# Three edits to one kernel: two stores moved behind loads on one DMA queue, and one product moved to another PSUM tile

## The chip, the cores and the metric

The kernel runs on one core of a Trainium2 chip. A core has a matrix engine (TensorE, PE in the profile), a vector engine (VectorE, DVE), a scalar engine (ScalarE, ACT), GpSimd (POOL) and a sync engine (SP). Every transfer of this kernel is issued from SP, which takes its instructions strictly one after the other: one that waits holds all that stand behind it. The metric is the device time of one execution in microseconds, and lower is better.

## The reference

One decoder layer over 1024 positions of width 1024, in float32. Three blocks, each added to the running sum h, and a last RMSNorm:

```
h = h + concat(pool(p), sgu(u, v)) @ w_out          # p, u, v = rmsnorm(h) @ w_in
q = (rmsnorm(h) @ wq), k = (memn @ wk), v = (memn @ wv)   # memn = rmsnorm(mem), 256 memory rows
h = h + softmax(q k' / 16) v @ wo                   # 4 heads of 256
hc = conv_b + sum_k conv_w[k] * shift(rmsnorm(h) @ w_up, k)   # causal, 3 taps, 5632 channels
gate, val = split(hc)
h = h + (silu(gate) * val) @ w_down
```

## The kernel before

**How products are made.** Each operand is split into a high part (a cast on ACT, `split`, L151 or L154) and a low part (a subtraction on DVE, L152 or L155), and each product is three matmuls (`mm3`: high by high, high by low, low by high). All matmuls are recorded at L137, all loads at L158. The order of PE and of SP is the order in which the program is written. The order of ACT and DVE is written by hand in some stages and set by a scheduler in others; the stages of this change are of the second sort, with splits of weights at raised priority.

**Memory products** (`mem_proj`, L599). Before them the first block's output product ends. It has accumulated in four single-bank PSUM tiles named `sm` (four buffers in rotation) and two double-bank tiles named `big` (two buffers). DVE adds these tiles to the residual rows `res` (`add_res`, L438). Between them stands a small product into a `big` tile (`mem_row`, L535). Then `mem_proj` makes keys and values of the memory: eight streamed weight matrices each for `wk` and `wv`, two to a PSUM tile, 24 matmuls of 256 columns each. The first two matrices of `wk` are split ahead of time (`mem_first`).

**The heads' products** (`B_head`, L639). For i = 0 to 7, the values of one head times half of that head's rows of `wo`: 12 matmuls of 512 columns. `wo` comes as eight matrices of 512 KB into four buffers in rotation (raw0, raw1, tb2, tb3); matrix i + 3 is asked for at the start of step i, and its buffer is free when matrix i - 1 has been split. The split results go to two pairs of buffers in turn (wb0 and wb1, wb2 and wb3), so that the split of matrix i + 2 waits for the products of step i. ACT copies the result from PSUM to a tile `f` (L652). In steps 0 to 3 (heads 1 and 3) `f` is also stored to memory (`bf`, L654), to be read back in a later stage; steps 4 to 7 write into the same tiles `f` again. Behind the heads come the query products: eight matrices `wqT`, 24 matmuls of 256 columns each, through the same buffers.

**The up-projection** works on 11 chunks of 256 gate and 256 value channels. `pair(kind, c)` (L1011) makes the four blocks of one kind (0 gate, 1 value) of one chunk with seven products of 12 matmuls, `go(0)` to `go(6)`. `prepare` (L992) splits one of the seven weight combinations after each product, three products ahead, into wb0 to wb3 in rotation; at the first of each seven it issues four loads of 256 KB (`load_pair`, L834) into the halves of raw0 and raw1. The convolution (`conv_sum`, L963) is one ACT and two DVE instructions (L970 to L972) and leaves its sum in a buffer `h15`. `conv_gate` (L975) makes the Silu on ACT (L979) for gates, and for values the product with that Silu on DVE (L981), in place in a tile `h7`, which is stored to memory (`act`, L982). Chunk 0 is made apart, in ordinary products; pairs follow as (0,1), (1,1), (0,2), (1,2) and so on. The Silu of a chunk writes into the `h7` from which the chunk before was stored.

Of the kernel before, what the change touches and what calls it, by code (L numbers as in the profile page):

```python
# [29 lines left out]
def kernel(ctx: ExitStack, tc: tile.TileContext, a, out: bass.AP):  # L30
    nc = tc.nc
# [29 lines left out]
    def half(i, h):  # L61
        if i in slot:
            return slot[i][:, h * 1024 : (h + 1) * 1024]
        return hslot[i, h]
# [25 lines left out]
    def big():  # L90
        return psum.tile([P, 1024], F32, tag="big", name="big")

    def sm():
        return psum.tile([P, 512], F32, tag="sm", name="sm", bufs=4)
# [20 lines left out]
    def raw():  # L115
        r = raws[0][nraw[0] % len(raws[0])]
        nraw[0] += 1
        return r
# [3 lines left out]
    def wpair():  # L122
        i = nw[0] % 2
        nw[0] += 1
        return wb[2 * i], wb[2 * i + 1]
# [4 lines left out]
    def temp():  # L130
        t = tb[trange[0][nt[0] % len(trange[0])]]
        nt[0] += 1
        return t
# [5 lines left out]
    def mm3(o, lh, ll, rh, rl, start, stop, more=False):  # L139
        mm(o, lh, rh, start, False, more)  # L140
        mm(o, lh, rl, False, False, more)
        mm(o, ll, rh, False, stop, more)
# [6 lines left out]
    def split(src, hi, lo, scale=None):  # L149
        if scale is None:  # L150
            copied[0] = nc.scalar.copy(hi, src)  # L151
            nc.vector.tensor_tensor(lo, src, f32(hi), ALU.subtract)  # L152
        else:
            nc.scalar.activation(hi, src, AF.Copy, scale=scale)  # L154
            nc.vector.scalar_tensor_tensor(lo, src, scale, f32(hi), ALU.mult, ALU.subtract)  # L155
# [11 lines left out]
    def stream(src_ap, k, parts=1):  # L167

        r = raw()
        load(r.rearrange("p (k n) -> p k n", k=k), src_ap)  # L170
        hi, lo = wpair()
        with tc.high_priority():
            for q in range(parts):
                c = slice(q * 1024 // parts, (q + 1) * 1024 // parts)
                split(r[:, c], hi[:, c], lo[:, c])
        return (hi.rearrange("p (k n) -> p k n", k=k), lo.rearrange("p (k n) -> p k n", k=k))
# [34 lines left out]
    for kp in range(4):  # L211
        r, q = (raw().rearrange("p (k n) -> p k n", k=2) for _ in range(2))
# [24 lines left out]
    for k in range(KT):  # L237
        wh, wl = vw(k)
        xh, xl = xT(0, k)
        for t in range(4):  # L240
            c = slice(t * P, (t + 1) * P)
# [27 lines left out]
    for i in range(4, 8, 2):  # L269
        b = big()  # L270
        for j in range(2):
            c = slice((i + j - 4) * P, (i + j - 3) * P)
# [52 lines left out]
    def in_proj(m):  # L325
        pu_load(m + 1)
        r = pu_raw[m]
        hi, lo = wpair()
        with tc.high_priority():
            for q in range(2):  # L330
                c = slice(q * 512, (q + 1) * 512)
                split(r[:, c], hi[:, c], lo[:, c])
        wh, wl = (x.rearrange("p (k n) -> p k n", k=8) for x in (hi, lo))
        b = big()
        for t in range(2):
            for k in range(KT):
                xh, xl = xT(t, k)
                mm3(b[:, t * 512 : (t + 1) * 512], wh[:, k], wl[:, k], xh, xl, k == 0, k == KT - 1)
        return b
# [24 lines left out]
    for h in range(4):  # L364
        b = in_proj(h)
        if h == 0:

            R, dg = tb[0], temp()
            for q in range(2):
                rp = sm()  # L370
                for j in range(4):
                    i = 4 * q + j
# [8 lines left out]
        for q in range(2):  # L381
            zp = sm()
            for j in range(4):
                c = 4 * q + j
# [43 lines left out]
    for g in (3, 2, 1):  # L428
        b = in_proj(4 + (3 - g))
# [4 lines left out]
    b = in_proj(7)  # L434
# [112 lines left out]
    mem_first = []  # L547
# [50 lines left out]

    def mem_proj(w, dst):  # L599
        for q in range(4):  # L600
            b = sm()
            for j in range(2):
                wh, wl = mem_first.pop(0) if mem_first else stream(w[2 * q + j], 8)
                for k in range(KT):
                    mm3(b[:, j * M : (j + 1) * M], wh[:, k], wl[:, k], memT[0][:, k], memT[1][:, k], k == 0, k == KT - 1)
            t = temp()[:, :512]
            nc.vector.tensor_tensor(
                t.rearrange("p (j m) -> p j m", j=2),
                b.rearrange("p (j m) -> p j m", j=2),
                Rm.rearrange("p (o m) -> p o m", o=1).broadcast_to([P, 2, M]),  # L610
                ALU.mult,
            )
            t = t.rearrange("p (j m) -> p j m", j=2)
            split(t, dst[0][:, 2 * q : 2 * q + 2], dst[1][:, 2 * q : 2 * q + 2])

    mem_proj(a["wk"], kT)
    mem_proj(a["wv"], vT)


    bf = [[dram.tile([P, 1024], F32, tag=f"bf{j}_{n}", name=f"bf{j}_{n}") for n in range(2)] for j in range(2)]  # L620
# [5 lines left out]

    heads = [(n, h) for h in (1, 3, 0, 2) for n in range(2)]
    wo_raw = []

    def wo_load():  # L630
        if len(wo_raw) < len(heads):
            n, h = heads[len(wo_raw)]
            wo_raw.append(raw())
            load(wo_raw[-1].rearrange("p (k n) -> p k n", k=2), a["wo"][n, h])
# [4 lines left out]
    def B_head(i):  # L639
        wo_load()  # L640
        n, h = heads[i]
        hi, lo = wpair()
        with tc.high_priority():
            split(wo_raw[i], hi, lo)
        wh, wl = (w.rearrange("p (k n) -> p k n", k=2) for w in (hi, lo))
        f = half(6 + h // 2, n)
        for mt in range(2):
            b = sm()
            c = slice(mt * P, (mt + 1) * P)
            for j in range(2):  # L650
                mm3(b, vT[0][:, 2 * h + j, c], vT[1][:, 2 * h + j, c], wh[:, j], wl[:, j], j == 0, j == 1)
            nc.scalar.copy(f[:, mt * 512 : (mt + 1) * 512], b)  # L652
        if h % 2:
            nc.sync.dma_start(bf[h // 2][n], f)  # L654

    for i in range(8):
        B_head(i)
# [46 lines left out]
    for dt in range(KT):  # L704
# [5 lines left out]
        else:  # L710
            b = big()
# [116 lines left out]
    def hl(t):  # L828
        return t[:, :512], t[:, 512:]
# [123 lines left out]
    def product(o, w, name, start=True, stop=True, more=False):  # L953
        wh, wl = (blk4(x) for x in hl(w))
        for k in range(4):
            xh, xl = xb(name, k)
            mm3(o, wh[:, k], wl[:, k], xh, xl, start and k == 0, stop and k == 3, more)
# [5 lines left out]
    def conv_sum(kind, c, j):  # L963

        h, f = H[kind][j], kind * NF + 2 * c + j
        w = lambda q: pconv[:, f, q : q + 1]
        o = half(15, ntv[0] % 2)
        ntv[0] += 1
        stt = nc.vector.scalar_tensor_tensor
        nc.scalar.activation(o, h, AF.Identity, bias=w(3), scale=w(2))  # L970
        stt(o[:, 1:], h[:, : S - 1], w(1), o[:, 1:], ALU.mult, ALU.add)  # L971
        stt(o[:, 2:], h[:, : S - 2], w(0), o[:, 2:], ALU.mult, ALU.add)  # L972
        return o

    def conv_gate(kind, c, j, o):  # L975

        sg = half(7, j)
        if kind == 0:
            nc.scalar.activation(sg, o, AF.Silu)  # L979
        else:  # L980
            nc.vector.tensor_tensor(sg, sg, o, ALU.mult)  # L981
            nc.sync.dma_start(act[c][j], sg)  # L982

    def conv(kind, c, j):
        conv_gate(kind, c, j, conv_sum(kind, c, j))
# [25 lines left out]
    def pair(kind, c, after=None):  # L1011
        X, Z, Y, V = val if kind else bank
        (c11, c12), (c21, c22) = (hl(H[kind][j]) for j in range(2))
        add = lambda o, x: nc.vector.tensor_tensor(o, o, x, ALU.add)  # L1014

        def go(q, o, xname, start=True):
            product(o, ready.pop((kind, c, q)), xname, start, True, not start)
            prepare()
            if after is not None:
                after(q)  # L1020

        go(0, X, "B11")
        nc.scalar.copy(c11, X)  # L1023
        go(1, Z, "B21")
        add(c11, Z)
        go(2, X, "T2", False)
        nc.scalar.copy(c21, X)
        go(3, Y, "T3")
        add(c21, Y)
        go(4, X, "T1", False)  # L1030
        nc.scalar.copy(c22, X)
        add(c22, Y)
        go(5, V, "T4")
        add(c21, V)
        conv(kind, c, 1)
        go(6, X, "B22", False)
        nc.scalar.copy(c12, X)
        conv(kind, c, 0)
# [15 lines left out]
    both = range(2)  # L1054
# [35 lines left out]
    sums0 = [conv_sum(0, 0, 0)]  # L1090
# [13 lines left out]
    for j in both:  # L1104
        conv_gate(0, 0, j, sums0[j])
    for j in both:
        conv(1, 0, j)

# [193 lines left out]
        at(67 + i, first_half, i)  # L1304

    for c in range(1, NC):
        pair(0, c)
        if c < NC - 1:
            pair(1, c)

# [10 lines left out]
    def add(o, x):  # L1321
        tt(o, o, x, ALU.add)
# [132 lines left out]
```

## Time and profile before

| | |
|---|---|
| median of 3 runs | 1157.74 us (1157.64 to 1158.26) |
| profiled execution, its own time | 1158.6 us |
| its span in the profile | 1156.9 us |
| PE busy | 1140.5 us |
| DVE busy | 859.6 us |
| ACT busy | 553.6 us |
| HBM read and written | 124.37 MB and 47.19 MB |

The span reaches from the first to the last instruction in the profile; the execution's own time is 1.7 us more. Busy time of PE counts a matmul until its modelled end, and two that follow each other overlap, so PE can read as busy while it runs below its best rate. The granted clock of TensorE in this execution has a mean of 0.999 of full speed.

### The profile page before, as it was taken

What the parts mean: (1) busy time and instruction counts of PE and PEld (TensorE: products, weight loads), DVE (VectorE), ACT (ScalarE), POOL (GpSimd) and SP (SyncE); (2) the same over time, 40 slices, a digit from 0 to 9 for tenths busy, and PEclk for the clock granted to TensorE, in tenths of its full rate; (3) what the DMA queues carried; (4) which work ended last, traced back from release to release, by engine and by line L of the source; (5) the groups of instructions that cost most, each with busy time, mean ns of one, the idle gap of its engine ahead of it and who ended that gap; (6) DMA issues with size and microseconds to landing.
All of it is one profiled execution on the core that took longest, in us unless ns stands there. A gap on an engine that the chain in (4) does not pass through costs nothing.

```text
span 1156.9 us, 14416 instructions
## 1 busy us (share of the span) xinstructions
PE 1140.5 (99%) x5416; PEld 956.2 (83%) x5416; DVE 859.6 (74%) x1114; ACT 553.6 (48%) x843; POOL 36.9 (3%) x75
## 2 busy tenths in 40 slices
PE   9999999999999999999999999999999999999997
PEld 7888888899788888888878888888888888888886
DVE  5776866566687336767887878787888878988695
ACT  7633222355764333447555545554454553334454
POOL 1200300100000000000000000000000000000000
PEclk9999999999999999999999999999999999999999
DMA  9688536645678126510212222232213297313111
GB/s 349 249 317 295 203 132 245 242 146 168 239 272 310 50 103 224 196 61 1 73 59 87 100 83 74 73 110 82 82 56 109 74 353 265 109 37 128 64 73 73
DMA packets 62278, 172.50 MB, mean 149 GB/s; under 512 B 7040, under 2 KB 7168, under 8 KB 62208
## 3 DMA queue, kind: packets, MB, share of 16 engines
q1 hardware_dynamic: 62208, 171.58, 41.3%
q8 instruction: 42, 0.69, 0.2%
q14 instruction: 28, 0.23, 0.1%
HBM read 124.37 MB, written 47.19 MB: 148 GB/s over the span
## 4 chain that ended last, share of the span: by engine, by line
PE 94%; DVE 3%; DMA 1%; ACT 1%; issue 1%; SPq 0%; ACTq 0%; DVEq 0%
PE sm L137 39%; PE bank L137 27%; PE big L137 26%; PE sm L145 2%; DVE wb L152 1%; DMA raw<-in_wo_dram 1%; DVE h L971 0%; DMA raw<-in_w_up_dram 0%; ACT wb L151 0%; DMA h<-in_w_v_dram 0%; DVE h L972 0%; DVE h L981 0%; DVE h L152 0%; ACT h L970 0%; DVE raw L999 0%
## 5 line engine op out<-in xcount | busy, mean ns | idle before, releaser
L137 PE MATMUL sm<-slot,wb 128*128 128x512 f32 (+1 forms) x1208 | 234.0, 347 | 3.3 <-DVE res L438 1.2
L137 PEld LDWEIGHTS sm<-slot,wb 128*128 128x128 f32 x1208 | 194.4, 189 | 32.6 <-ACT wb L151 1.5
L151 ACT CAST wb<-raw 128x512 fp32r<-128x512 f32 (+1 forms) x162 | 104.6, 653 | 205.5 <-PE sm L137 55.5
L137 PE MATMUL big<-slot,wb 128*128 128x512 f32 (+1 forms) x728 | 185.9, 378 | 0.0
L137 PE MATMUL bank<-slot,wb 128*128 128x512 f32 x728 | 175.2, 389 | 0.5 <-ACT tb L1023 0.5
L137 PEld LDWEIGHTS bank<-slot,wb 128*128 128x128 f32 x728 | 136.6, 188 | 29.2 <-ACT tb L1023 0.9
L152 DVE TENSOR_TENSOR wb<-raw,wb 128x512 fp32r<-128x512 f32 (+1 forms) x162 | 116.7, 727 | 52.9 <-ACT wb L151 52.8
L137 PEld LDWEIGHTS big<-slot,wb 128*128 128x128 f32 x728 | 129.9, 188 | 25.1 <-DVE tb L404 0.7
L137 PE MATMUL big<-h,wb 128*128 128x512 f32 x160 | 62.3, 389 | 0.0
L151 ACT CAST slot<-slot 128x1024 fp32r<-128x1024 f32 x31 | 32.2, 1050 | 61.7 <-PE big L137 22.8
L971 DVE SCALAR_TENSOR_TENSOR h<-tb,par,h 128x1023 f32<-128x1023 f32 x42 | 53.8, 1281 | 9.5 <-ACT h L970 8.6
L152 DVE TENSOR_TENSOR slot<-slot,slot 128x1024 fp32r<-128x1024 f32 x31 | 37.8, 1223 | 28.4 <-ACT slot L151 26.9
L137 PE MATMUL big<-slot,slot 128*128 128x512 f32 x224 | 54.5, 390 | 0.0
L137 PE MATMUL bank<-tb,tb 128*128 128x512 f32 x176 | 54.2, 389 | 0.0
L137 PE MATMUL bank<-wb,wb 128*128 128x512 f32 x176 | 54.2, 389 | 0.0
L151 ACT CAST wb<-slot 128x1024 fp32r<-128x1024 f32 (+1 forms) x35 | 29.5, 856 | 51.1 <-PE bank L137 19.9
L970 ACT ACTIVATE h<-tb,par 128x1024 f32<-128x1024 f32 x42 | 52.3, 1245 | 3.2 <-DVE tb L1014 2.6
L972 DVE SCALAR_TENSOR_TENSOR h<-tb,par,h 128x1022 f32<-128x1022 f32 x42 | 53.7, 1278 | 0.1
L137 PE MATMUL sm<-slot,slot 128*128 128x512 f32 x216 | 51.9, 400 | 1.2 <-ACT slot L151 1.2
L137 PEld LDWEIGHTS sm<-slot,slot 128*128 128x128 f32 x216 | 41.6, 193 | 10.7 <-ACT slot L151 1.5
L137 PE MATMUL sm<-h,wb 128*128 128x512 f32 x184 | 50.0, 389 | 0.0
L137 PEld LDWEIGHTS big<-slot,slot 128*128 128x128 f32 x224 | 42.0, 188 | 8.7
(214 smaller groups left out, 1898.8 us busy)
## 6 DMA issues: line engine op xcount, KB each, us to landing
raw<-in_w_up_dram SPq DMA_DIRECT2D x88, 256.0 KB, 3.6
wf<-res SPq DMA_DIRECT2D x28, 512.0 KB, 3.6
wfa<-slot SPq DMA_DIRECT2D x28, 512.0 KB, 3.5
act<-h SPq DMA_DIRECT2D x22, 512.0 KB, 3.0
h<-wf SPq DMA_DIRECT2D x20, 512.0 KB, 4.1
slot<-act SPq DMA_DIRECT2D x33, 256.0 KB, 4.9
slot<-in_w_down_dram SPq DMA_DIRECT2D x33, 256.0 KB, 5.3
res<-in_x_dram SPq DMA_DIRECT2D x16, 512.0 KB, 9.2
```

The source lines that it names most:

```text
L137: i = nc.tensor.matmul(o, l, r, start=start, stop=stop, skip_group_check=more)
L145: i = nc.tensor.transpose(o, i_, ident)
L151: copied[0] = nc.scalar.copy(hi, src)
L152: nc.vector.tensor_tensor(lo, src, f32(hi), ALU.subtract)
L970: nc.scalar.activation(o, h, AF.Identity, bias=w(3), scale=w(2))
L971: stt(o[:, 1:], h[:, : S - 1], w(1), o[:, 1:], ALU.mult, ALU.add)
L972: stt(o[:, 2:], h[:, : S - 2], w(0), o[:, 2:], ALU.mult, ALU.add)
```

## The change

Three edits. The stores of the four tiles `f` are issued two steps later than before. The first pair of memory products goes to half of a `big` tile (a double bank) in place of an `sm` tile. For chunk 0, the product of the convolved values with the Silu, and its store, are taken out from behind their convolution sum and put into pair (0,1), after its fifth product and what `prepare` issues there.

```diff
     def mem_proj(w, dst):
         for q in range(4):
-            b = sm()
+
+            b = big()[:, :512] if mem_first else sm()
...
     heads = [(n, h) for h in (1, 3, 0, 2) for n in range(2)]
     wo_raw = []
+    kept = []
...
             nc.scalar.copy(f[:, mt * 512 : (mt + 1) * 512], b)
-        if h % 2:
-            nc.sync.dma_start(bf[h // 2][n], f)
+        kept.append((bf[h // 2][n], f) if h % 2 else None)
+
+        if i >= 2 and kept[i - 2]:
+            nc.sync.dma_start(*kept[i - 2])
...
     for j in both:
         conv_gate(0, 0, j, sums0[j])
     for j in both:
-        conv(1, 0, j)
+        sums0[j] = conv_sum(1, 0, j)
+
+    def values_out(q):
+
+        if q == 4:
+            for j in both:
+                conv_gate(1, 0, j, sums0[j])
...
     for c in range(1, NC):
-        pair(0, c)
+        pair(0, c, values_out if c == 1 else None)
```

How this moves instructions, at three places. First the SP queue at the heads: loads of `wo` and stores of the four tiles (`slot6` in two halves, `h7_0`, `h7_1`), with the first loads of `wqT` behind them.

```order
 L158 DMA tb3_1273<-in_wo_dram 128x1024
-L654 DMA bf0_0_2168<-slot6_2200 128x1024
 L158 DMA raw0_73<-in_wo_dram 128x1024
-L654 DMA bf0_1_2169<-slot6_2200 128x1024
 L158 DMA raw1_74<-in_wo_dram 128x1024
-L654 DMA bf1_0_2170<-h7_0_2201 128x1024
+L658 DMA bf0_0_2168<-slot6_2200 128x1024
 L158 DMA tb2_1272<-in_wo_dram 128x1024
-L654 DMA bf1_1_2171<-h7_1_2202 128x1024
+L658 DMA bf0_1_2169<-slot6_2200 128x1024
 L158 DMA tb3_1273<-in_wo_dram 128x1024
+L658 DMA bf1_0_2170<-h7_0_2201 128x1024
```

The loads of matrices 4 (raw0) and 5 (raw1) no longer stand behind a store, those of 6 and 7 stand behind one that is two steps older; the fourth store, behind the last row shown, is now the last instruction ahead of the loads of `wqT`.

On ACT the scheduler's order changes with it. Steps 5 to 7 of the heads: casts of matrices 6 (from tb2) and 7 (from tb3), copies of results (`sm` into `slot6`), and one cast of another kind (`slot4` from `slot6`, the first of the combinations that a later stage needs, which waits for the products of step 5).

```order
 L151 CAST wb0_75<-tb2_1272 128x1024
-L652 COPY slot6_2200<-sm_2307 128x512
+L654 COPY slot6_2200<-sm_2295 128x512
+L654 COPY slot6_2200<-sm_2306 128x512
 L151 CAST slot4_83<-slot6_2200 128x1024
-L652 COPY slot6_2200<-sm_2315 128x512
 L151 CAST wb2_77<-tb3_1273 128x1024
```

The cast of matrix 7 now follows the one into `slot4` at once; one copy that stood between them stands behind. Further up, at the memory products, the cast of the third `wk` matrix (wb0 from tb2) moves ahead of one square of a residual row (L162), with no other move there on ACT.

Third, the SP queue at chunk 1 of the up-projection, from the last load of the stage before and the four loads of pair (0,1) on, before:

```order
L158 DMA h13_1_1709<-wfa5_1_1_2195 128x1024
L158 DMA raw0_73<-in_w_up_dram 128x512 x2
L158 DMA raw1_74<-in_w_up_dram 128x512 x2
L982 DMA act0_0_3950<-h7_0_4300 128x1024
L982 DMA act0_1_3951<-h7_1_4302 128x1024
L158 DMA raw0_73<-in_w_up_dram 128x512 x2
L158 DMA raw1_74<-in_w_up_dram 128x512 x2
```

and in the change:

```order
L158 DMA h13_1_1709<-wfa5_1_1_2195 128x1024
L158 DMA raw0_73<-in_w_up_dram 128x512 x2
L158 DMA raw1_74<-in_w_up_dram 128x512 x2
L158 DMA raw0_73<-in_w_up_dram 128x512 x2
L158 DMA raw1_74<-in_w_up_dram 128x512 x2
L986 DMA act0_0_3950<-h7_0_4300 128x1024
L986 DMA act0_1_3951<-h7_1_4302 128x1024
```

The four loads of pair (1,1) have changed places with the two stores of chunk 0. On DVE the two products of L981 have moved down past the splits of pair (1,1)'s first matrices, and on ACT those matrices' casts have moved up.

## Rows read from the trace of the kernel before

**Rows 1.** Page, part 1: busy us, share of the span, instructions, by engine.
```profile
PE 1140.5 (99%) x5416; PEld 956.2 (83%) x5416; DVE 859.6 (74%) x1114; ACT 553.6 (48%) x843; POOL 36.9 (3%) x75
```

**Rows 2.** Timeline, all engines, around the first memory product (columns: start, duration).
```profile
226.63 1.27 DVE L438 TENSOR_TENSOR res<-res,big 128x512 f32<-128x512 f32 x2
...
230.29 0.60 PE L137 MATMUL big<-misc,ones 128*128 128x128 f32 x4
...
232.10 8.14 PE L137 MATMUL sm<-slot,wb 128*128 128x256 f32 x66 [1.20 <-DVE res L438]
...
234.13 1.04 ACT L162 ACTIVATE tb<-res 128x1024 f32<-128x1024 f32 x1
...
235.18 1.03 ACT L151 CAST wb<-tb 128x1024 fp32r<-128x1024 f32 x1
```

**Rows 3.** Timeline, TensorE alone, the heads' products from first to last.
```profile
278.24 11.29 PE L137 MATMUL sm<-wb,slot 128*128 128x512 f32 x49
...
289.72 2.83 PE L137 MATMUL sm<-wb,slot 128*128 128x512 f32 x11 [0.19 <-DVE wb L152]
...
293.46 0.49 PE L137 MATMUL sm<-wb,slot 128*128 128x512 f32 x1 [0.91 <-ACT wb L151]
...
294.72 5.77 PE L137 MATMUL sm<-wb,slot 128*128 128x512 f32 x24 [0.77 <-DVE wb L152]
...
301.19 2.79 PE L137 MATMUL sm<-wb,slot 128*128 128x512 f32 x11 [0.70 <-DVE wb L152]
...
303.82 2.44 PE L137 MATMUL big<-slot,wb 128*128 128x256 f32 x19
```

**Rows 4.** Timeline, other engines and the SP queue, in the same stretch.
```profile
279.40 1.22 DVE L152 TENSOR_TENSOR wb<-raw,wb 128x1024 fp32r<-128x1024 f32 x1 [0.27 <-ACT wb L151]
...
285.46 0.33 SPq L654 DMA_DIRECT2D bf<-slot  x1
286.22 0.33 SPq L158 DMA_DIRECT2D raw<-in_wo_dram  x1
...
292.37 1.04 ACT L151 CAST wb<-raw 128x1024 fp32r<-128x1024 f32 x1 [2.44 <-DMA raw<-in_wo_dram]
...
297.40 1.05 ACT L151 CAST slot<-slot 128x1024 fp32r<-128x1024 f32 x1 [0.63 <-PE sm L137]
...
298.83 1.05 ACT L151 CAST wb<-tb 128x1024 fp32r<-128x1024 f32 x1
...
303.79 1.23 DVE L152 TENSOR_TENSOR slot<-slot,slot 128x1024 fp32r<-128x1024 f32 x1 [1.45 <-PE sm L137]
```

**Rows 5.** Chain that ended last: one product pair later on, 84 matmuls.
```profile
617.04 19.04 PE sm L137 x84
```

**Rows 6.** Timeline, all engines, chunk 1 of the up-projection.
```profile
565.08 5.05 SPq L982 DMA_DIRECT2D act<-h  x2
...
566.16 0.69 DVE L152 TENSOR_TENSOR wb<-raw,wb 128x512 fp32r<-128x512 f32 x1
...
570.23 18.79 SPq L158 DMA_DIRECT2D raw<-in_w_up_dram  x8
...
574.28 0.62 ACT L151 CAST wb<-raw 128x512 fp32r<-128x512 f32 x1 [2.82 <-DMA raw<-in_w_up_dram]
...
576.11 5.60 PE L137 MATMUL sm<-slot,wb 128*128 128x512 f32 x24
...
580.33 1.06 ACT L979 ACTIVATE h<-h 128x1024 f32<-128x1024 f32 x1
...
582.81 0.73 PE L137 MATMUL sm<-slot,wb 128*128 128x512 f32 x2 [1.10 <-ACT wb L151]
...
597.84 8.32 PE L137 MATMUL bank<-slot,wb 128*128 128x512 f32 x36
```

**Rows 7.** Stretch of query products: length, PE, PEld, DVE, ACT, POOL busy, clock, DMA, GB/s.
```profile
307.00:311.00 4.00, 4.00 (x35) 4.00 (x35) 4.00 (x6) 4.00 (x7) 0.00 (x0) 1.00 0.76 230
```

**Rows 8.** DMA issues around chunk 1: KB each, median us from issue to landing.
```profile
act<-h SPq DMA_DIRECT2D x2, 512.0 KB, 2.8
```

## The prediction

> **What bounds the kernel now.** The page comes first: PE is busy for 1140.5 of the 1156.9 us of the span [rows 1]. An edit that leaves the matmuls as they are, as this one does, can win only time that PE loses, and part of the missing 16.4 us is the program's beginning and end. So the second view is the timeline of PE, read for brackets (an idle time and who ended it) and for groups that take longer than their matmuls need. The measure of need is a stretch without a wait: one pair of the up-projection late in the chain takes 19.04 us for 84 matmuls of 512 columns, 0.227 us each [rows 5]; 12 matmuls, one step of the heads or one product of a pair, are 2.72 us.
>
> Three places touched by the diff lose time by that measure.
>
> *Memory products.* The small product into `big` ends at 230.29 + 0.60 = 230.89; the first memory product starts at 232.10, held by DVE's eviction of `sm` [rows 2]. Lost: 1.21 us.
>
> *Heads.* From 278.24 to the first query product at 303.82 are 25.58 us, for 96 matmuls that need 21.76 [rows 3, 5]. Lost: 3.82 us, more than the brackets add up to (2.57), because PE also counts as busy while a matmul drains. The first four steps run at full pace (49 matmuls in 11.29); the loss lies at steps 4, 5 and 7. At step 5 the cause is a load: ACT stood idle 2.44 us for a `wo` matrix whose load was issued at 286.22, behind a store at 285.46, and reached ACT at 292.37, 6.15 us later [rows 4]. At steps 4 and 7 the loads were there and ACT's order was at fault: at step 7 it cast `slot4`, then copied a result, then at 298.83 cast the matrix that PE needed [rows 4].
>
> *Pair (1,1).* From 576.11 to the next pair at 597.84 are 21.73 us against 19.04 [rows 5, 6]. Lost: 2.69 us, at its third product, which at 582.81 got a matrix split late [rows 6]. On SP two stores of chunk 0 stand ahead of this pair's loads: the queue was held from 565.08, the loads began at 570.23, and ACT waited 2.82 us for the first, until 574.28 [rows 6].
>
> **The change part by part.** No instruction is added or dropped; all three edits move or rename.
>
> *The double bank.* Half of the `big` tile that the product now takes was last evicted in the two operations from 226.63 that end by 227.9 [rows 2], 3 us before PE is free for it. So PE should start at about 230.9. Next it needs the third `wk` matrix 5.9 us later (66 matmuls of 256 columns took 8.14, so 48 take 5.9), at 236.8. Its cast stood at 235.18 behind a square begun at 234.13; in the new order it has that square's place, and with 1.03 for the cast and 1.22 for the low part it is done at about 236.4 [rows 2, 4]. I take the whole 1.2 us. Below: had the cast kept its place, the matrix would be complete at 237.5 and 0.5 us would be left. If the tile were not free, nothing.
>
> *Stores of the heads behind the loads.* The buffer of matrix 5 is free when matrix 1 has been split, at 279.40 + 1.22 = 280.6 [rows 4]. With no store ahead the load can start there, 5.6 us earlier than at 286.22; even with the crowded 6.15 us it lands by 286.8. Its cast has to wait anyway for the end of step 3, about 289.1 + 0.2, so the load is covered by 2.5 us. Matrices 6 and 7 stand behind stores whose data were ready two steps earlier. Cast and subtraction then take 1.05 + 1.22, ending at about 291.6, and step 5 is due at 291.8: this holds at a spare of 0.2 us, as in steps 0 to 3, which did it without a wait. What is late next is step 7: the cast into `slot4` still stands ahead of the cast of matrix 7, but it now follows at 297.40 + 1.05 = 298.45 instead of 298.83 [rows 4]. The wait there, 301.19 less the 300.16 at which 24 matmuls from 294.72 end, is 1.03; 0.38 less leaves 0.65 [rows 3, 4]. Gain: 3.82 - 0.65, about 3.2 us. Above: 3.8. Below: step 5 alone lost 294.72 - 289.72 less its 12 matmuls, 2.28; if each of the steps 5 to 7 came 0.3 us late by the spare of 0.2 failing, 1.4 would be left.
>
> The stores themselves move later by two steps; steps 4 to 7 write the same tiles and must wait for them. The first is issued near 282.7 (a step of 2.72 before the second, 285.46) and step 4's first copy comes half a step after its start at 289.1, near 290.5: 8 us, for a transfer that took 6.15 when crowded. The fourth store, two steps after the second, at about 291, now stands ahead of the first `wqT` load; that matrix is needed at 278.24 + 21.76 = 300.0, and 6.15 us of landing leave 3 us.
>
> *Chunk 0's values.* The four loads wait no longer for the gating products but for their buffers. The last buffer is read last by the subtraction at 566.16, so it is free at 566.9; with the 4.05 us from 570.23 to 574.28 its load lands by 571, before even the first one did [rows 6]. The combinations and splits for the third product then start some 5 us earlier than they did, against a lateness of 2.7. The cover is wide, so the wait should go. But ACT and DVE get a new order here. Laying the durations end to end in it, the copies that free X for the third and fifth products of pair (1,1) end only 0.3 to 0.6 us ahead of their turns. I take 0.2 us for that: gain 2.5 us. Bounds: 2.7 and, if the new order stalls as long as the old one, 0.
>
> **The sum.** 1.2 + 3.2 + 2.5 = 6.9 us. The profiled execution took 1158.6 us, its span 1156.9, so it would come to 1151.7; on the median of 1157.74, which lies 0.9 below it, 1150.8. All later stages have no dependence on absolute time: they shift as a whole.
>
> **The rivals.**
>
> *DVE gives the heads' gain back* (1154.0). The stage behind the heads leaves DVE no idle time: 4.00 of 4.00 us [rows 7]. If DVE were its bound, PE arriving 3.2 us earlier would only wait there. Against: DVE's first work there starts at 303.79 after waiting 1.45 us for PE's last head [rows 4], so DVE's stretch is tied to PE's and shifts with it, in an unchanged order. Chance 0.10.
>
> *Pair (1,1) trades one wait for another* (1153.3). ACT is in order; a cast waiting for its buffer now stands ahead of copies that free X. For it: the thin spares above. Then the third term is 0. Chance 0.14. This and the one before together, about 1156: 0.04.
>
> *Slower: the store holds the Silu.* The Silu of chunk 1 writes where the store of chunk 0 reads. It ran at 580.33 [rows 6]; the second store, issued near 570 before, moves to about 574, and took 2.8 us [rows 8], so it is done 3 us ahead. Behind the Silu on ACT stands the copy for the fifth product, so beyond that point every microsecond of landing costs one. To end over 0.2% above the old time it would have to land some 15 us after issue (6 of cover, 7 of gain, 2 beyond). Landings here do vary, from 2.8 to the 6.15 of the heads, but not so far: chance 0.03.
>
> The Trainium skill states the mechanism of this rival in "DMA: Bandwidth & Descriptors", section "Anatomy of one DMA — SWDGE (gpsimd) path": the fixed part of a transfer is mostly the receipt for the last byte written, which the page says can be a surprisingly long delay when the target is HBM, as it is for these stores. By its fit, 2.0 us plus bytes over 436 GB/s, a 512 KB store would take an estimated 3.2 us and end about 577, and the sum would be the same; the trace's 2.8 us [rows 8] is shorter still. By that rule a delay is to be feared, by the row it is not, and the row decides.
>
> *The waits are only relabelled* (1157.7, no change): other work stands ready behind each. Nothing in the three places shows it; 0.04.
>
> **How the numbers follow.** My forecast, with all three terms in their bounds, has 0.65: 1150.8, within 1149.6 (all waits gone, 7.7, and 0.4 for measurement) and 1152.5. The range for 8 in 10 takes in the two single rivals, each of which loses one term: to 1154.4. A measurement of this kernel can tell about 0.2%, 2.3 us, so faster means below 1155.4: 0.65 + 0.10 + 0.14 = 0.89. Within 0.2%: 0.04 + 0.04 = 0.08. Slower: 0.03.
>
> **What the profile after would show.** The first memory product should follow the small product at 230.9 with no bracket for `res`. Steps 0 to 6 of the heads should be one run of PE without a bracket, step 7 a wait of 0.5 to 0.8 on DVE's low part, and the whole stretch 22.4 us, not 25.6. No ACT idle time should be ended by a `wo` load. On SP, four `w_up` loads should start between 559 and 567 (less the 4.4 us by which everything has shifted), ahead of two stores near 572 and 574, and pair (1,1) should take 19.0 to 19.4 us. I am wrong if the query products after the heads last longer than before, if pair (1,1) shows a bracket after copies of X or a Silu, or if waits appear at a place that the diff does not touch.

## The result and the profile after

| | before | after |
|---|---|---|
| median of 4 runs | 1157.69 us (1156.8 to 1158.26) | 1151.12 us (1149.63 to 1152.18) |
| ratio, with its 95% interval | | 0.9935 [0.992, 0.995] |
| profiled execution, its span | 1156.9 us | 1147.9 us |

The change takes 6.57 us off the median; 6.9 were forecast. On another chip, in the repeats below, it took 10.75 us off, so a median alone does not say what the edits are worth. Page, part 1 of the changed kernel, which answers to [rows 1]:

```profile
PE 1137.1 (99%) x5416; PEld 955.0 (83%) x5416; DVE 859.1 (75%) x1114; ACT 552.7 (48%) x843; POOL 36.9 (3%) x75
```

The instruction counts are those of before. PE's busy time fell by only 3.4 us where the span fell by 9.0: a PE that waits can read as idle or as busy. Lengths are therefore compared from the start of one group of matmuls to the start of another.

**First memory product.** Timeline of the changed kernel (start, duration), to be held against [rows 2]:

```profile
227.76 0.60 PE L137 MATMUL big<-misc,ones 128*128 128x128 f32 x4
...
228.12 6.00 PE L137 MATMUL big<-slot,wb 128*128 128x256 f32 x48
...
231.60 1.03 ACT L151 CAST wb<-tb 128x1024 fp32r<-128x1024 f32 x1
...
232.66 1.23 DVE L152 TENSOR_TENSOR wb<-tb,wb 128x1024 fp32r<-128x1024 f32 x1 [0.78 <-ACT wb L151]
...
233.96 4.24 PE L137 MATMUL sm<-slot,wb 128*128 128x256 f32 x34
```

The bracket for `res` is gone. The product starts 0.36 us after the small one where it started 1.81 after it: a gain of 1.45. The third matrix is complete at 232.66 + 1.23 = 233.89, and the product that uses it goes on at 233.96, with no bracket.

**Heads.** The same view, against [rows 3, 4]:

```profile
274.27 19.46 PE L137 MATMUL sm<-wb,slot 128*128 128x512 f32 x85
...
285.38 1.05 ACT L151 CAST wb<-raw 128x1024 fp32r<-128x1024 f32 x1 [0.70 <-PE sm L137]
...
290.65 1.05 ACT L151 CAST slot<-slot 128x1024 fp32r<-128x1024 f32 x1 [0.53 <-PE sm L137]
291.60 1.04 ACT L151 CAST wb<-tb 128x1024 fp32r<-128x1024 f32 x1
...
292.68 1.23 DVE L152 TENSOR_TENSOR wb<-tb,wb 128x1024 fp32r<-128x1024 f32 x1 [2.27 <-ACT wb L151]
...
293.96 2.83 PE L137 MATMUL sm<-wb,slot 128*128 128x512 f32 x11 [0.23 <-DVE wb L152]
...
296.63 3.04 PE L137 MATMUL big<-slot,wb 128*128 128x256 f32 x24
```

Steps 0 to 6 and the first matmul of step 7 (85 in all) are one run. The cast of matrix 5, which had waited 2.44 us for its load, now waits for PE, as the casts of earlier steps do. What remains is step 7: cast into `slot4`, cast of matrix 7, low part, and only then the matmuls. The stretch is 296.63 - 274.27 = 22.36 us, against 25.58.

**Pair (1,1).** The same view, against [rows 6]:

```profile
552.67 7.05 SPq L158 DMA_DIRECT2D raw<-in_w_up_dram  x4
...
563.63 0.62 ACT L151 CAST wb<-raw 128x512 fp32r<-128x512 f32 x1 [2.26 <-DMA raw<-in_w_up_dram]
...
564.14 2.93 SPq L986 DMA_DIRECT2D act<-h  x2
...
568.93 8.32 PE L137 MATMUL sm<-slot,wb 128*128 128x512 f32 x36
...
572.88 0.57 ACT L1027 COPY tb<-sm 128x512 f32<-128x512 f32 x1
573.39 1.06 ACT L983 ACTIVATE h<-h 128x1024 f32<-128x1024 f32 x1
...
587.98 4.24 PE L137 MATMUL bank<-slot,wb 128*128 128x512 f32 x18
```

The four loads are issued from 552.67 on, ahead of the two stores. ACT still stands idle 2.26 us for one of them, but at 563.63, five microseconds before PE begins the pair, and PE waits for nothing: 587.98 - 568.93 = 19.05 us against 21.73.

The profile's 9.0 us exceed what the edits give. The chain's first stage, 96 matmuls before the first product into a `big` tile, starts 1.07 us earlier and is 1.46 us shorter, 2.53 in all, and nothing in it was edited. Over the profiles below it lasts 22.4 to 24.2 us: 22.4 in both of the changed kernel, 23.9 and 24.0 in both of the kernel before, but also 23.6 to 24.2 in e5, e6 and e7, which hold all three edits. Why is open. Against that, pair (1,4) takes 19.54 us in place of 19.04, and 0.3 are lost at the end. 2.53 + 1.45 + 3.22 + 2.68 - 0.5 - 0.3 = 9.1, the span's 9.0 within rounding. Without the first stage some 6.5 remain. That this is also the difference of the medians proves nothing: the medians hold the first stages of executions that were not profiled.

### The profile page after: what moved, and what is told of

It is laid out like the page before. It is cut to its first block, busy times and chain, and to the rows that moved or that the text cites. A ratio compares the mean times of both kernels' runs of the same rounds, so it can differ in the third digit from the quotient of the medians.

```text
span 1147.9 us, 14414 instructions
## 1 busy us (share of the span) xinstructions
PE 1137.1 (99%) x5416; PEld 955.0 (83%) x5416; DVE 859.1 (75%) x1114; ACT 552.7 (48%) x843; POOL 36.9 (3%) x75
## 4 chain that ended last, share of the span: by engine, by line
PE 95%; DVE 2%; ACT 1%; DMA 1%; issue 1%; SPq 0%; ACTq 0%; DVEq 0%
PE sm L137 39%; PE bank L137 28%; PE big L137 27%; PE sm L145 2%; DMA raw<-in_w_up_dram 1%; ACT wb L151 0%; DVE wb L152 0%; DMA h<-in_w_v_dram 0%; DVE raw L1003 0%; DVE h L975 0%; ACT h L974 0%; DVE h L152 0%; DVE slot L152 0%; SPq L158 0%; DVE slot L1292 0%
## 5 line engine op out<-in xcount | busy, mean ns | idle before, releaser
L137 PE MATMUL sm<-slot,wb 128*128 128x512 f32 (+1 forms) x1160 | 227.9, 350 | 0.2 <-ACT tb L1027 0.2
L137 PEld LDWEIGHTS sm<-slot,wb 128*128 128x128 f32 x1160 | 188.7, 189 | 29.0 <-ACT tb L1027 0.6
L137 PE MATMUL big<-slot,wb 128*128 128x512 f32 (+1 forms) x776 | 191.9, 372 | 0.0
L137 PEld LDWEIGHTS big<-slot,wb 128*128 128x128 f32 x776 | 135.7, 189 | 25.1 <-DVE tb L404 0.7
```

The costliest lines, as they stand in the source:

```text
L137: i = nc.tensor.matmul(o, l, r, start=start, stop=stop, skip_group_check=more)
```

## Experiments

The table has each run's median and its ratio to the kernel before on the same chip, and four stages of its profile: from the small product to the first memory product, the heads, and pairs (1,1) and (1,4), each from the start of its first group to the start of the next stage's. The kernel before had medians of 1159.22 us beside the first four runs, 1159.08 beside the next four, and 1159.91 beside e9 and the repeat; the last two rows are single runs.

| run | us | ratio, 95% interval | memory | heads | (1,1) | (1,4) |
|---|---|---|---|---|---|---|
| before | 1157.69 | 1 | 1.81 | 25.58 | 21.73 | 19.04 |
| after | 1151.12 | 0.9935 [0.992, 0.995] | 0.36 | 22.36 | 19.05 | 19.54 |
| e1: heads' stores | 1155.19 | 0.9963 [0.9948, 0.9977] | 1.81 | 22.31 | 23.39 | 19.04 |
| e2: double bank | 1158.06 | 0.9986 [0.9975, 0.9998] | 0.36 | 27.19 | 21.51 | 19.04 |
| e3: values | 1154.78 | 0.9959 [0.9943, 0.9974] | 1.81 | 25.65 | 19.04 | 19.62 |
| e4: other queue | 1152.96 | 0.9942 [0.9927, 0.9957] | 1.81 | 22.31 | 19.04 | 19.04 |
| e5: stores first | 1154.96 | 0.9966 [0.9953, 0.9979] | 0.36 | 22.34 | 22.51 | 19.69 |
| e6: halves | 1150.54 | 0.9924 [0.9908, 0.9939] | 0.36 | 21.79 | 19.04 | 19.62 |
| e7: all chunks | 1152.05 | 0.9939 [0.9922, 0.9955] | 0.36 | 22.33 | 19.04 | 19.04 |
| e8: one step | 1149.46 | 0.992 [0.9904, 0.9935] | 0.36 | 22.33 | 19.04 | 19.36 |
| e9: e6 and e7 | 1148.32 | 0.9909 [0.9893, 0.9925] | 0.36 | 21.78 | 19.05 | 19.04 |
| after, again | 1149.16 | 0.991 [0.9896, 0.9924] | 0.36 | 22.31 | 19.05 | 19.05 |
| e2, again | 1159.4 | | 0.36 | 27.39 | 21.65 | 19.80 |
| before, again | 1160.2 | | 1.81 | 25.82 | 21.88 | 19.51 |

The theory: SP takes its queue in order, and a store that waits for its data holds the loads behind it; each part of the change removes such a hold or, in the double bank, one wait for an eviction. The rivals are the transfers themselves (stores and loads that share the DMA engines slow each other, and the change only parts them in time) and the new order on ACT and DVE, which the scheduler makes for each of these kernels.

### The parts one by one: e1, e2, e3

The three parts of the diff shown above, each alone in the kernel before.

> The kernel before with the stores of the heads two steps later, and nothing else. Theory (the loads of wo were held in SP's queue behind stores): the heads take 22.4 us from first to last as in the changed kernel, not 25.6; the first memory product still starts 1.8 us after the small one, pair (1,1) still takes 21.7; the time falls by 3.2 us, ratio 0.997. Rival (the gain in the heads is lent by the other two edits, which start PE earlier or change ACT's order): the heads keep part of their 3.8 us of loss. If the three edits work apart, the three kernels that do one each gain 1.45, 3.2 and 2.7 us and their sum is that of the change.

> The kernel before with the first memory product in a double bank, and nothing else. Theory: the product starts 0.4 us after the small one instead of 1.8, nothing else moves: heads 25.6, pair (1,1) 21.7, ratio 0.9987 (1.45 us), not to be told from 1 by the time. Rival (what is won there is waited for again at the heads' loads, which hang on SP): the heads grow to 27 us and the time stays.

> The kernel before with chunk 0's gating products and stores moved into pair (0,1), and nothing else. Theory: pair (1,1) takes 19.05 us instead of 21.73, heads 25.6, first memory product 1.8 us after the small one; ratio 0.9977. Rival (the wait goes elsewhere without the other edits): pair (0,1) or a later pair takes longer than 19.8 or 19.04.

In e1 the heads take 22.31 us, in e3 pair (1,1) takes 19.04, in e2 the memory product starts 0.36 us after the small one: the gain of a part does not need the other two. The times fall too, by 0.37, 0.14 and 0.41%; those of e1 and e3 by more than their stages give (4.0 and 4.4 us against 3.3 and 2.7), so the times alone do not share out the gain. In e3 pair (1,4) takes 19.62 us, as its rival has it, but so it does in kernels without this edit (see the table).

The heads in e2 take 27.19 us, 1.6 more than before, in a stage that this kernel does not edit. That is the number of the rival, but not its mechanism: PE does not wait longer for loads. Timeline of TensorE in e2, against [rows 3]:

```profile
288.09 2.79 PE L137 MATMUL sm<-wb,slot 128*128 128x512 f32 x11 [0.25 <-DVE wb L152]
291.83 0.50 PE L137 MATMUL sm<-wb,slot 128*128 128x512 f32 x1 [0.95 <-ACT wb L151]
293.09 7.35 PE L137 MATMUL sm<-wb,slot 128*128 128x512 f32 x24 [0.76 <-DVE wb L152]
301.12 2.79 PE L137 MATMUL sm<-wb,slot 128*128 128x512 f32 x11 [0.68 <-DVE wb L152]
```

The brackets are those of before within 0.06 us, but the 24 matmuls take 7.35 us where they took 5.77. Windows of 1 us of e2 (busy time and instructions of PE, PEld, DVE, ACT and POOL, then PEclk, DMA share, GB/s):

```profile
292.00:293.00 1.00, 0.33 (x1) 0.02 (x1) 1.00 (x1) 0.75 (x2) 0.00 (x0) 1.00 1.01 414
293.00:294.00 1.00, 0.91 (x3) 0.80 (x4) 0.04 (x1) 0.72 (x1) 0.00 (x0) 0.81 1.03 422
294.00:295.00 1.00, 1.00 (x4) 0.71 (x4) 0.64 (x1) 0.33 (x1) 0.00 (x0) 0.50 1.05 418
295.00:296.00 1.00, 1.00 (x4) 0.81 (x3) 0.59 (x1) 0.59 (x1) 0.00 (x0) 0.50 1.04 414
296.00:297.00 1.00, 1.00 (x4) 0.81 (x3) 0.00 (x0) 0.00 (x0) 0.00 (x0) 0.50 0.94 332
297.00:298.00 1.00, 1.00 (x6) 0.75 (x6) 0.00 (x0) 0.68 (x1) 0.00 (x0) 0.99 0.84 291
```

The granted clock is 0.50 in three windows, the lower level (1.2 of 2.4 GHz). The view counts 4 matmuls in each, where at the full clock it counts 6; those that only reach into a window count too. In the kernel before, the same view after nearly the same waits:

```profile
293.00:294.00 1.00, 0.49 (x1) 0.19 (x1) 0.56 (x1) 1.00 (x3) 0.00 (x0) 1.00 1.00 410
294.00:295.00 1.00, 0.28 (x1) 0.28 (x2) 0.67 (x1) 0.46 (x2) 0.00 (x0) 1.00 1.07 438
295.00:296.00 1.00, 1.00 (x6) 0.78 (x6) 0.00 (x0) 0.97 (x1) 0.00 (x0) 1.00 0.97 397
296.00:297.00 1.00, 1.00 (x6) 0.82 (x5) 1.00 (x1) 0.59 (x1) 0.00 (x0) 1.00 1.07 438
```

The length of the waits does not decide it. In e3 each of the three is within 0.03 us of that in e2, and the 24 matmuls take 5.73 us:

```profile
290.19 2.79 PE L137 MATMUL sm<-wb,slot 128*128 128x512 f32 x11 [0.26 <-DVE wb L152]
293.97 0.50 PE L137 MATMUL sm<-wb,slot 128*128 128x512 f32 x1 [0.98 <-ACT wb L151]
295.23 5.73 PE L137 MATMUL sm<-wb,slot 128*128 128x512 f32 x24 [0.76 <-DVE wb L152]
```

So the double bank alone wins 1.45 us at its own place, and its profile loses 1.6 at the heads. e1 has a fall of this kind at pair (1,1): a granted clock of 0.50 to 0.69 between 582 and 586, behind the waits of 1.12 and 1.02 us that this kernel keeps, where 10 matmuls took 4.15 us, in before 2.56 behind waits of 1.10 and 1.02; the pair takes 23.39 us instead of 21.73.

### Is it the queue or the transfers? e4

The kernel before, written in its own order, with the four stores of the heads and the two of chunk 0 issued by GpSimd:

```diff
         if h % 2:
-            nc.sync.dma_start(bf[h // 2][n], f)
+            nc.gpsimd.dma_start(bf[h // 2][n], f)
...
-            nc.sync.dma_start(act[c][j], sg)
+            (nc.gpsimd if c == 0 else nc.sync).dma_start(act[c][j], sg)
```

> The kernel before, all in its old places, but the four stores of the heads and the two of chunk 0 are issued from GpSimd's queue, so that nothing on SP waits for them while the bytes move as early as before. Theory (SP's queue was what held the loads): heads 22.4 to 22.8 us and pair (1,1) 19.0 to 19.4, as in the changed kernel; together 5.9 us faster. Rival (the stores' bytes beside the loads make the loads late): the heads keep over 24.5 us, since the stores run just when they did, and only the pair gains.

Timeline of e4 at the heads:

```profile
277.76 19.46 PE L137 MATMUL sm<-wb,slot 128*128 128x512 f32 x85
...
282.60 0.72 POOL L654 DMA_DIRECT2D bf<-slot  x1 [44.92 <-ACT slot L652]
283.10 2.99 SPq L158 DMA_DIRECT2D tb<-in_wo_dram  x2
...
285.27 0.54 POOL L654 DMA_DIRECT2D bf<-slot  x1 [1.95 <-ACT slot L652]
...
287.98 0.53 POOL L654 DMA_DIRECT2D bf<-h  x1 [2.17 <-ACT h L652]
288.49 3.05 SPq L158 DMA_DIRECT2D raw<-in_wqT_dram  x2
...
290.70 0.53 POOL L654 DMA_DIRECT2D bf<-h  x1 [2.18 <-ACT h L652]
```

The stores leave as soon as their data are there, between the loads, and steps 0 to 6 are one run all the same; both stages are as short as in the changed kernel (22.31 and 19.04 us). The stores' bytes, moved as early as before, cost nothing that PE shows once no load waits behind them. Traffic is not quite out of it: the loads now leave earlier, and that of matrix 5 took 3.5 us from issue to landing where it took 6.1 in the kernel before.

The rival of the order on ACT and DVE is not settled by this. The scheduler answered the edit with another order: on ACT it is that of the changed kernel, at the heads and around chunk 1, and on DVE the second gating product moved down behind pair (1,1)'s first splits. ACT at step 7, then that product:

```profile
294.14 1.05 ACT L151 CAST slot<-slot 128x1024 fp32r<-128x1024 f32 x1 [0.53 <-PE sm L137]
295.09 1.04 ACT L151 CAST wb<-tb 128x1024 fp32r<-128x1024 f32 x1
...
566.05 1.22 DVE L981 TENSOR_TENSOR h<-h,h 128x1024 f32<-128x1024 f32 x1
```

What the order could have done can be read from the kernel before. At step 5 the load landed at 292.29, and the cast began at 292.37 [rows 4]; with 1.05 and 1.22 the matrix is complete at 294.64, and PE goes on at 294.72 [rows 3]. No order is faster with that load, so the 2.28 us lost at step 5 are that load's. It was late in two ways, issued 5.6 us after its buffer was free and 6.1 us on its way, and by estimate it took both: with 3.5 us it would have landed at 289.8, the matrix complete at 292.0, ahead of the step's turn at 289.72 + 2.72 = 292.44; and in e8 the loads of matrices 6 and 7, not held, took 5.6 and 5.7 us without a loss. The other 0.94 of the heads' gain lie at steps 4 and 7, where ACT's order changed too.

At pair (1,1) the third of the four loads landed at 575.92. From there the third product needs three combinations on DVE, begun 0.60 us apart, a cast of 0.62 and a low part of 0.69; done at once, they would be ready near 579.2 by estimate, and the product's turn was 576.11 + 24 x 0.227 = 581.56. DVE did two passes of the convolution and three splits in between, and PE began at 582.81. There the held loads and the order behind them made the loss together, and no run parts the two: none keeps the hold and puts that work first.

### Stores ahead of loads again: e5

The changed kernel, with chunk 0's values one product earlier, so that on SP the stores stand ahead of the loads once more:

```diff
     def values_out(q):
 
-        if q == 4:
+        if q == 3:
```

> The changed kernel with chunk 0's gating products and stores one product earlier in pair (0,1), after its fourth product, so that on SP both stores stand again ahead of pair (1,1)'s four loads. Theory (the place on SP decides): the loads start after the second gating product as before, near 563 on the changed kernel's scale instead of from 553 on, and pair (1,1) takes over 21 us, not 19.05. Rival (the new order of the splits on DVE and ACT is what helps): the pair stays under 19.8.

Timeline of e5 at chunk 1:

```profile
563.90 1.46 SPq L986 DMA_DIRECT2D act<-h  x2
565.47 19.06 SPq L158 DMA_DIRECT2D raw<-in_w_up_dram  x8
...
572.59 5.28 PE L137 MATMUL sm<-slot,wb 128*128 128x512 f32 x22 [0.68 <-DVE wb L152]
...
579.24 0.73 PE L137 MATMUL sm<-slot,wb 128*128 128x512 f32 x2 [1.37 <-ACT wb L151]
580.39 2.57 PE L137 MATMUL sm<-slot,wb 128*128 128x512 f32 x10 [0.42 <-DVE wb L152]
```

The loads begin at 565.47 instead of 552.67, 5.7 us ahead of the pair instead of 16.3, and the pair takes 22.51 us. Moving the gating products is thus not enough: with the stores ahead of the loads, it costs about what it cost before (21.73). ACT and DVE get another order here too, nearer to that of the kernel before. The first load landed 3.75 us after its issue, at 569.22, and ACT cast it only at 570.52, behind an instruction of the convolution; the wait of 0.68 at the start of the pair is one that before did not have. So e5 does not part hold and order either. Over all profiles the long pair goes with the held loads (before, e1, e2, e5 and the repeats of before and e2), and the short one with loads that are not held.

### What is left at step 7: e6

At step 7 the cast into `slot4` stands ahead of matrix 7's. e6 swaps the two halves of that one form, so that its cast writes a buffer that the heads read to their end and must come behind them:

```diff
         hi, lo = halves(4 + nform[0] % 2)
+        if (cc, s) == (0, 0):
+            hi, lo = lo, hi
```

> The changed kernel with high and low part of the first combination of the next stage exchanged in slot4's two halves, so that its cast cannot start before the last head's products and no longer stands ahead of the cast of matrix 7. Theory (that cast is what makes step 7 late): the bracket of 0.23 us at step 7 goes, and the heads take 21.8 to 21.9 us instead of 22.36; ratio to before 0.993, not to be told from the changed kernel by the time. Rival (step 7 is late for another reason, or the displaced cast is paid for in the query products): heads 22.3 or more, or the stretch from the heads' end to the first transposes longer than 20.15 us.

Timeline of e6:

```profile
277.18 21.95 PE L137 MATMUL sm<-wb,slot 128*128 128x512 f32 x96
...
299.01 1.04 ACT L151 CAST slot<-slot 128x1024 fp32r<-128x1024 f32 x1
```

All 96 matmuls are one run, 21.79 us to the next group, 0.227 each; the cast stands behind them. The wait of 0.2 us before step 7 has gone, and with it the whole remainder of the heads, 0.5 to 0.6 us. The wait of 0.6 us at the first transposes has gone as well: from the first query product to pair (0,1) pass 204.71 us instead of 205.41. The time, 1150.54, differs from the changed kernel's by less than can be told.

### The other chunks, and the distance: e7, e8

In every later chunk the values' stores still stand ahead of the next pair's loads. e7 treats them all as the change treats chunk 0; e8 issues the heads' stores one step later instead of two.

```diff
+    def values_of(c):
+        def out(q):
+            if q == 4:
+                for j, o in late.pop(c):
+                    conv_gate(1, c, j, o)
+        return out
...
-        pair(0, c, values_out if c == 1 else None)
+        pair(0, c, values_of(c - 1))
```

```diff
-        if i >= 2 and kept[i - 2]:
-            nc.sync.dma_start(*kept[i - 2])
+        if i >= 1 and kept[i - 1]:
+            nc.sync.dma_start(*kept[i - 1])
```

> The changed kernel with the same move for every chunk: each chunk's gating products and stores stand behind the loads of the next value pair. In two profiles so far pair (1,4) took 19.54 and 19.62 us where its first load landed late. Theory (SP holds the value pairs' loads in every chunk, just short of being late): ACT's idle time that a w_up load ends, up to 5.8 us per value pair, falls to under 1 us, all pairs take 19.04, and the time is that of the changed kernel less at most 0.5. Rival (the later chunks need the old order on DVE and ACT, since the Silu then waits for the store): some pairs take longer than 19.2 and the time rises by over 1 us.

> The changed kernel with the heads' stores one step later instead of two. ACT's order is the same but for one row. Theory (a load must not stand behind a store whose data is not yet there): a store one step late finds its data ready about when SP gets to it, so the loads of matrices 5 to 7 start at most 0.5 us later than in the changed kernel, with 2.5 us to spare: heads 22.3 to 22.5 us. Rival (two steps are needed): heads over 23 us.

ACT's waits for loads of `w_up`, over the whole execution (us in total, times, longest), in the changed kernel:

```profile
ACT wb L151 <- DMA raw<-in_w_up_dram: 41.6, 18, 5.8
```

and in e7:

```profile
ACT wb L151 <- DMA raw<-in_w_up_dram: 2.3, 1, 2.3
```

39 us of these waits go, and the time does not move: 1152.05 (1151.82 to 1152.18), a ratio of 0.9939 where the changed kernel had 0.9935. ACT is idle for PE instead. Its casts' waits for products into `bank` tiles, in the changed kernel and then in e7:

```profile
ACT wb L151 <- PE bank L137: 71.8, 49, 2.4
...
ACT wb L151 <- PE bank L137: 110.3, 76, 2.4
```

Nearly all of the 39 us was idle time of an engine that PE did not wait for. One of these waits does reach PE: the longest, 5.8 us, is the late load that makes pair (1,4) 19.54. In e7 all pairs are at 19.04. A loss of 1 us elsewhere, as the rival has it, is not excluded by the time: e6 and e8 had 1150.54 and 1149.46 on the same chip.

The traces also show that a hold bunches the loads behind it. In the changed kernel the four loads of each value pair from chunk 2 on leave within 2.1 us once the stores are out, and take 3.6 to 4.5 us each to land, at chunk 4 6.0 to 6.4; in e7 they leave one by one over 10.9 us, as their buffers come free, and take 2.5 to 3.0. In e8 the heads take 22.33 us, as with two steps, so one step is distance enough.

### Together, and three repeats: e9

e9 is the changed kernel with the edits of e6 and e7. Beside it ran the changed kernel once more; e2 and the kernel before were profiled a second time, in one execution each.

> The changed kernel with both mends that the profiles bore out: the exchanged halves of the first combination (heads 21.79 us) and every chunk's stores behind the next value pair's loads (all pairs 19.04). Theory: the two add up, heads 21.8, all pairs 19.04, no bracket at the transposes; 0.6 us from the heads and about 0.5 from pair (1,4), so 1.0 to 1.2 us under the changed kernel on the same chip, ratio to before 0.992 to 0.993. Rival (the order that the scheduler makes for both together brings a wait back): a pair over 19.2 or the heads over 22.2.

> The changed kernel as it is, a second time, on the same chip as the combined version. Theory: first memory product 0.36 us after the small one, heads 22.3 to 22.4, pair (1,1) 19.05, whatever the execution; what varies between executions lies in the first 96 matmuls (22.4 to 24.2 us so far) and in single late loads. Ratio 0.993 to 0.994.

> The double bank alone a second time. In the first profile its heads took 27.19 us, of which 1.6 lay in a stretch where TensorE's clock was granted at half. Theory (the clock took it, not the edit): without such a stretch the heads take 25.6 us and the 1.45 us are kept. Rival (PE only waits longer at the heads for what it won): 27 us again at the full clock.

> The kernel before a second time, for the spread of its stages: heads 25.6, pair (1,1) 21.5 to 21.7 unless the clock falls behind one of the two waits, which adds 1.6 us there (seen in two of the four profiles that still had the wait at its old length); first stage 22.4 to 24.2.

e9 and the changed kernel, on one chip: 1148.32 (1148.11 to 1150.6) and 1149.16 us (1149.07 to 1149.21). The heads of e9 are 0.53 us shorter, the stretch behind them 0.7, and ACT waits for no `w_up` load; the difference of 0.84 us in the time lies within the spread, so e9 is the better kernel by its stages and not proven so by its time. The second profile of e2 fell to the half clock at the same place, 293 to 296, and its heads took 27.39 us; what e2 gains without that fall no profile shows. In the kernel before, neither profile shows it at the heads (25.58 and 25.82), nor does e3's (25.65).

In this set the changed kernel is 10.75 us below the kernel before, a ratio of 0.991 [0.9896, 0.9924], not the expected 0.993 to 0.994 and more than the 7.35 us of the three places. The granted clock says where part of it may lie. Of the 14 profiles, the five with a stretch at half clock ahead of the program's last microseconds (e1, e2, e3 and the second ones of e2 and of before) have a mean clock of 0.996 or 0.997, all others 0.998 or 0.999. Of the 35 executions of the kernel before beside the experiments, 22 had 0.997 or less; of the changed kernel's eight, one; of e2's first twelve, ten. The two of e2 at 0.998 took 1155.02 and 1155.26 us, some 3 below its median. So taking the waits away seems to save falls of the clock as well; how much of the 10.75 us that makes was not measured.

## Why the prediction was right, step by step

- **Double bank, 1.2 us.** Measured 1.45. The tile was free, and the cast had moved in time, as worked out. The error is in the term's size: the 0.60 us shown for the small product was counted as work, but the next product starts 0.36 us after it begins. The end of a group of matmuls is modelled and includes their draining.
- **Heads, 3.2 us.** Measured 3.22, and 3.27 in e1. Steps 5 and 6 lost their waits on a spare estimated at 0.2 us. The residual at step 7 was forecast as 0.65, and the stretch stands 22.36 - 21.76 = 0.60 above its need. Its bracket shows only 0.23, below the forecast 0.5 to 0.8, so length and not brackets is the measure here too. e6 confirms the cause given: with the cast into `slot4` behind the heads the residual is gone.
- **Chunk 0's values, 2.5 us.** Measured 2.68. That held loads were the whole cause was not shown: the order on DVE behind them had its part (e4). The loads were issued from 552.67 to 559.40, 2 to 3 us ahead of the forecast, which counted a shift of 4.4 us where the pair came 7.2 earlier. The 0.2 us kept back for copies that free X was not needed: the copy for the third product ended at 573.45, 0.9 us before that product's turn at 568.93 + 24 x 0.227 = 574.38.
- **The sum.** 1.45 + 3.22 + 2.68 = 7.35 against 6.9, less 0.5 at pair (1,4) and 0.3 at the end, which the prediction did not have. The late pair has a wait of 0.21 us at a place that the diff does not touch, one of the prediction's own signs of being wrong. It is not the change's: it shows in the second profile of before (19.51) and not in the second of the changed kernel (19.05). In all, it is late in 7 of the 12 profiles that have later chunks' stores ahead of loads, and in neither of the two with e7's order. That the medians came so near to 6.9 is in part luck: the first stage varies by up to 1.8 us between profiles, and on the second chip the medians differ by 10.75.
- **DVE gives the heads' gain back: refuted.** From the first query product to the first transposes pass 20.15 us before and after: that stage shifted as a whole. **Pair (1,1) trades waits: refuted** at 19.05 us; it has no bracket after a copy or a Silu.
- **The store holds the Silu: refuted.** The second store was issued near 566.7 and landed 2.6 us later, at 569.4, and even the first Silu, at 573.39, did not wait for one.
- **Relabelled waits: refuted** in all three places by the brackets that are gone. Only ACT's 2.26 us at 563.63 is such a wait, and it reaches nobody.

What the prediction did not ask is whether a wait that it removes costs more than its own length. At the full clock it does not, and both profiles it was made from and judged by had the full clock at these places; e1 and e2 show that this is not always so. The 6.9 us hold no term for it.

Three things stay open: how hold and order share the gain at pair (1,1) and at steps 4 and 7; why the bunched loads of `w_up` land later still at chunk 4 (6.0 us from issue at 673.01 in the changed kernel, where the 256 KB loads at chunk 1 took 2.6 to 4.1); and why e2 fell to the half clock twice behind waits that before went through at the full clock.

## What to carry to other kernels

Where one queue issues everything in order, look for a store that waits for its data ahead of a load that could go. Moving it one step back, or to another engine's queue, was worth 3.2 and 2.7 us here, together with the order that the scheduler made for it; a store beside loads that are not held cost nothing that PE showed. Where a scheduler orders the other engines, compare its order before and after every edit: an edit of one queue is not an edit of that queue alone. Before doing the same everywhere, ask whether the engine that the loads feed is waited for: 39 us of ACT's idle time were worth half a microsecond at most. And measure a stage from start to start: brackets and busy shares of a pipelined engine hide part of what it loses.

## What the runs showed of the hardware

A wait of TensorE can cost twice. Behind waits of 0.25, 0.95 and 0.76 us the granted clock fell to the lower level for some 3.4 us in e2, 24 matmuls took 7.35 us instead of 5.77, and the stage lost 1.6 us beyond its waits. Behind waits of 0.26, 0.98 and 0.76 us in e3, and of 0.19, 0.91 and 0.77 in the kernel before, it stayed at the full clock. The fall came in both profiles of e2, in e1's pair (1,1) and, near 8 us, at the start of e1, e3 and the second profile of before, and in none at a place whose waits were gone. What decides was not found; it is not the length of these waits.

Loads held behind a store leave in a bunch and take longer to land: 256 KB in 3.6 to 4.5 us, where the same loads spread over 10.9 us took 2.5 to 3.0 (the changed kernel and e7; 6.0 to 6.4 at chunk 4).

Stores of 512 KB issued by GpSimd took 0.53 to 0.72 us of that engine each in e4, and ran beside SP's loads without a wait on PE that the changed kernel does not have.
